# A hybrid attention layer on one core: the seams between the MLP's token blocks, with the last norm's scale, shift and store deferred, a fourth token tile landed early, and the first two weight pieces split apart

## The chip, the cores and the metric

The kernel runs on one core of a Trainium2 chip. The metric is the device time of one execution in microseconds (us), lower is better; where several executions were timed, their median. The engines are named as in the profile: PE is TensorE's matmul (PEld its weight load), DVE is VectorE, ACT is ScalarE, POOL is GpSimd, SP is SyncE, which here only issues DMAs. "ACTq" and "SPq" are DMA issues on the queues of ACT and SP. Each engine works through its own instructions in the order in which they stand.

## The reference

One inference step of one decoder layer in fp32: 2048 prompt tokens and 64 new tokens of 8 running sequences, model width 1024, hidden width 4096. A joint projection feeds softmax attention with forget gates (8 heads of 64; the new tokens read a paged cache of 8192 positions) and an mLSTM (4 heads of 128). Their outputs go through `w_o`, a first layer norm, the MLP and a second one. The part that matters here:

```python
mix = jnp.concatenate([fox_h, mn.astype(x.dtype)], axis=-1) @ w_o
x1 = _layer_norm(DN_ALPHA * x + mix, ln1_g, ln1_b)
hid = jnp.square(jax.nn.relu(x1 @ w1))
return _layer_norm(DN_ALPHA * x1 + hid @ w2, ln2_g, ln2_b)
```

`_layer_norm` subtracts the mean, divides by the root of variance plus epsilon, multiplies by `g` (the scale) and adds `b` (the shift).

## The kernel before, in words

Every large product is done in three passes (`mm3`): both operands are split into a rounded upper half (`split_hi`, an ACT copy, L149) and the rest (`split_lo`, a DVE subtraction, L152), and PE adds upper × upper (L157), upper × lower (L158) and lower × upper (L159). So each weight piece that arrives by DMA (`wr`, 512 KB) costs one ACT operation (`wh`) and one DVE operation (`wl`) before PE can use all of it, and each token tile likewise (`x1h`, `x1l`).

The work comes in phases: the projection, the mLSTM, prompt attention, phase O (`w_o` and the first norm for 16 tiles of 128 prompt tokens; it stores x1 to a scratch tensor, `dx` in the profile and `dx1` in the code) and phase C, the MLP. Phase C takes the tokens in four blocks: tiles 0 to 3, 4 to 7, 8 to 11, and 12 to 15 with the 64 new tokens as a fifth tile, numbered 16. I call the passages between them O→C, 0→1, 1→2 and 2→3. In each block all weights pass once, in 16 slices of 256 hidden columns:

- `hidden(fc)` takes two w1 pieces of 512 rows each (`w1_pieces`), accumulates `ph` in PSUM on PE, and makes relu (ACT, L1392), square (ACT, L1393) and the split of the result (`hh` on ACT, `hl` on DVE). `hq`, the buffer between relu and split, has one copy; `ph` has three, shared with the transposes of token tiles.
- `output(fcs)` takes w2 pieces of 128 rows, accumulates `py` on PE for each tile and half of the columns, and DVE adds it to the tile's output row `y` (L1420 for the first slice, which loads the row from x1 by a DMA on ACT's queue, L1409; L1422 for the others). There are five output rows of 128 x 1024.
- After the last slice `layer_norm` follows tile by tile: statistics on DVE (L165 to L167, L169), a power on POOL (L168), the normalisation on ACT (L170), the scale on DVE (L171), the shift on POOL (L172), and the store to `y_prompt` on SP (L1426).

While the last slice of a block runs, `load(ci + 1)` brings the next block's token tiles: a load on SP into one of two landing buffers (`xr`, L1213), eight transposes on PE (L1225), and the splits into `x1h` and `x1l`, which have one copy each for 576 tokens.

Raw weights have four buffers, which the norms' vectors `g` and `b` also use; `wh` has five and `wl` four.

Beside all this the new tokens' attention over the cache runs in steps (`tick`): indirect DMA gathers issued by POOL (`kT`, `vt`, `xr`), DVE transposes of the keys, short matmuls (`sQ`, `sT`, `sO`) and a custom DVE operation for the scores (L1633).

The code's order isn't the engines' order. A tile scheduler estimates when each instruction can start and orders every engine's queue by that and by priority, with dependences through buffers kept; `tc.issue_after` ties what stands in its scope behind a given instruction.

Of the kernel before, what the change touches and what calls it, by code (L numbers as in the profile page):

```python
# [10 lines left out]
F32 = mybir.dt.float32  # L11
# [3 lines left out]
OP = mybir.AluOpType  # L15
# [37 lines left out]
def body(ctx, tc, I, O, stages):  # L53
# [49 lines left out]
    last = {}  # L103
# [56 lines left out]

    def layer_norm(x, np_, g, b, wk, tg, eng=None):
        w = wk.tile([128, 64], F32, name="ln", bufs=2)
# [7 lines left out]
        A.activation(x, x, AF.Identity, bias=rs[:np_, 2:3], scale=rs[:np_, 1:2])  # L170
        V.tensor_tensor(x, x, g[:np_], op=OP.mult)  # L171
        (eng or G).tensor_tensor(x, x, b[:np_], op=OP.add)  # L172

# [1004 lines left out]
    def landing(n=128):  # L1178

        return pcw.tile([128, 1024], F32, name="xr", bufs=2)[:n]  # L1180
# [9 lines left out]
    C = {}  # L1190
# [13 lines left out]
    def row():  # L1204
        return C["py"].tile([128, D], F32, name="y", bufs=5)

    def w1_pieces(fc):
        return [piece(I["w1"][0][kg * 512:kg * 512 + 512, fc * 256:fc * 256 + 256].rearrange("(k p) c -> p k c", p=128)) for kg in range(2)]
# [21 lines left out]
    def phase_o(halves):  # L1230
# [94 lines left out]
        x1_turn(3, 3, nx[3], px_of)  # L1325
        C["w1"] = w1_pieces(0)
        end(15)
# [4 lines left out]
    def phase_c():  # L1332
# [30 lines left out]

        CB = [[0, 1, 2, 3], [4, 5, 6, 7], [8, 9, 10, 11], [12, 13, 14, 15, 16]]
        def load(ci):
# [4 lines left out]
        vx["more"] = landing  # L1370
        for ci, blk in enumerate(CB):
            W = sum(tok_n(t) for t in blk)
# [25 lines left out]
            def output(fcs):  # L1398
# [4 lines left out]
                for t in blk:  # L1403
# [20 lines left out]
                    if 15 in fcs and t < 16:  # L1424
                        layer_norm(ys[t], n, *gb, pc, "2")
                        SY.dma_start(O["y_prompt"][0, t * 128:(t + 1) * 128], ys[t])  # L1426
# [430 lines left out]
```

## Time and profile before

| | |
|---|---|
| median of 3 executions | 3372.51 us (3365.42 to 3375.61) |
| the profiled execution | 3382.94 us, its span 3381.2 us, mean granted clock 0.988 |
| PE busy | 3266.7 us, 97% of the span |
| DVE busy | 2145.9 us, 63% |
| ACT busy | 1413.8 us, 42% |
| POOL busy | 869.5 us, 26% |
| moved by DMA | 646.25 MB |

Phase C takes the span from about 1617 us to the end. An instruction's row in the profile gives its start, its duration, engine, line, and output and input tiles without their numbers; square brackets hold how long the engine had been idle before it and what released it.

### The profile page before, as it was taken

The page shows a single profiled execution, that of the slowest core. Times are in us where ns is not written, and L with a number is a line of the kernel's source. Part 1 is how long each engine was busy: PE and PEld are TensorE (multiplying, and loading weights), DVE is VectorE, ACT ScalarE, POOL GpSimd, SP SyncE. Part 2 cuts the span into 40 slices and gives each one's busy share as a digit, 9 for nine tenths or more (in the row PEclk, how much of TensorE's full clock was granted, in tenths as well). Part 3 has the DMA queues.
Part 4 walks back from the last instruction along what each step waited for, and adds up shares of the span by engine and source line. Part 5 has one row for each costly group of instructions (what it writes and reads, how often), then busy time and mean ns, then how long its engine had stood idle before and what let it go on. Part 6 is the DMA issues. An engine that isn't in the chain of part 4 may idle for free. (4 is left out here: it accounts for less than half of the span.)

```text
span 3381.2 us, 57759 instructions
## 1 busy us (share of the span) xinstructions
PE 3266.7 (97%) x21564; PEld 2623.4 (78%) x21564; DVE 2145.9 (63%) x5180; ACT 1413.8 (42%) x2989; POOL 869.5 (26%) x928
## 2 busy tenths in 40 slices
PE   9999999999999999999999999999999999999998
PEld 8998897787866667677777776777777777888886
DVE  5857567556478878655666667666676545644545
ACT  4444245334378888422332333232332323433332
POOL 0112122422332222365423324323243110100001
PEclk9999999999999999999999999999999999999999
DMA  5665765866652322587776768767678545532221
GB/s 172 165 189 179 221 206 180 292 212 219 227 166 81 90 76 61 209 283 245 286 249 244 247 226 299 254 234 270 209 258 289 198 164 160 168 103 83 87 76 66
DMA packets 427232, 646.25 MB, mean 191 GB/s; under 512 B 83148, under 2 KB 320016, under 8 KB 426056
## 3 DMA queue, kind: packets, MB, share of 16 engines
q1 hardware_dynamic: 350184, 363.22, 35.3%
q0 software_dynamic: 74304, 270.57, 21.8%
q10 hardware_dynamic: 2464, 8.78, 0.7%
q8 instruction: 170, 2.79, 0.3%
q14 instruction: 110, 0.90, 0.1%
HBM read 589.63 MB, written 52.83 MB: 190 GB/s over the span
## 5 line engine op out<-in xcount | busy, mean ns | idle before, releaser
L1422 DVE TENSOR_TENSOR y<-y,py 128x512 f32<-128x512 f32 (+1 forms) x475 | 320.5, 681 | 310.7 <-PE py L159 287.4
L149 ACT ACTIVATE wh<-wr 128x1024 fp32r<-128x1024 f32 x268 | 278.1, 1056 | 500.8 <-PE py L159 215.3
L159 PE MATMUL ph<-x1h,wl 128*128 128x512 f32 (+1 forms) x1280 | 452.9, 355 | 7.7 <-DVE wl L152 7.1
L157 PE MATMUL ph<-x1h,wh 128*128 128x512 f32 (+1 forms) x1280 | 454.9, 355 | 3.6 <-ACT wh L149 2.9
L1597 POOL DMA_INDIRECT kT<-cache_k,idxK x256 | 272.5, 1064 | 718.2 <-PE sQ L1626 657.7
L158 PE MATMUL ph<-x1l,wh 128*128 128x512 f32 (+1 forms) x1280 | 454.4, 355 | 0.0
L1603 DVE STREAM_TRANSPOSE kT<-kT 128x512 f32<-128x512 f32 x512 | 330.3, 685 | 177.1 <-DMA kT<-cache_k,idxK 170.5
L157 PE MATMUL py<-wh,hh 128*128 128x512 f32 (+1 forms) x1088 | 431.7, 399 | 6.8 <-DVE y L1420 4.0
L158 PE MATMUL py<-wl,hh 128*128 128x512 f32 (+1 forms) x1088 | 426.4, 392 | 0.6 <-issue 0.6
L159 PE MATMUL py<-wh,hl 128*128 128x512 f32 (+1 forms) x1088 | 426.3, 393 | 0.3 <-issue 0.3
L152 DVE TENSOR_TENSOR wl<-wr,wh 128x1024 fp32r<-128x1024 f32 x268 | 335.0, 1256 | 81.5 <-ACT wh L149 28.6
L157 PE MATMUL pm<-whi,xhT 128*128 128x256 f32 (+2 forms) x1088 | 319.0, 293 | 4.6 <-ACT whi L149 1.7
L158 PE MATMUL pm<-wlo,xhT 128*128 128x256 f32 (+2 forms) x1088 | 313.8, 289 | 0.8 <-DVE wlo L152 0.8
L159 PE MATMUL pm<-whi,xlT 128*128 128x256 f32 (+3 forms) x1088 | 313.5, 288 | 0.0
L157 PEld LDWEIGHTS ph<-x1h,wh 128*128 128x128 f32 x1280 | 241.8, 189 | 42.9 <-issue 5.2
L159 PEld LDWEIGHTS ph<-x1h,wl 128*128 128x128 f32 x1280 | 241.8, 189 | 43.0 <-DVE wl L152 9.4
L158 PEld LDWEIGHTS ph<-x1l,wh 128*128 128x128 f32 x1280 | 241.9, 189 | 36.9 <-issue 4.1
L157 PEld LDWEIGHTS py<-wh,hh 128*128 128x128 f32 (+1 forms) x1088 | 201.3, 185 | 64.4 <-issue 11.9
L159 PEld LDWEIGHTS py<-wh,hl 128*128 128x128 f32 (+1 forms) x1088 | 200.9, 185 | 52.7 <-issue 5.3
L158 PEld LDWEIGHTS py<-wl,hh 128*128 128x128 f32 (+1 forms) x1088 | 201.4, 185 | 40.6 <-issue 2.3
L157 PEld LDWEIGHTS pm<-whi,xhT 128*128 128x128 f32 (+1 forms) x1088 | 207.9, 191 | 13.7 <-issue 7.8
L1072 ACT ACTIVATE S<-S,mx 128x512 f32<-128x512 f32 (+2 forms) x320 | 207.8, 652 | 17.7 <-DVE mx L1060 16.6
(394 smaller groups left out, 6534.9 us busy)
## 6 DMA issues: line engine op xcount, KB each, us to landing
wr<-w SPq DMA_DIRECT2D x256, 512.0 KB
wra<-w_in SPq DMA_DIRECT2D x112, 512.0 KB
Rb<-dR SPq DMA_DIRECT2D x128, 128.0 KB
wr<-w_o SPq DMA_DIRECT2D x16, 512.0 KB
xr<-dmix SPq DMA_DIRECT2D x16, 512.0 KB
y<-x_prompt SPq DMA_DIRECT2D x16, 512.0 KB
dx<-y SPq DMA_DIRECT2D x16, 512.0 KB
xr<-dx SPq DMA_DIRECT2D x16, 512.0 KB
```

The costliest lines, as they stand in the source:

```text
L149: last["ACT"] = A.activation(dst, src, AF.Copy, scale=scale)
L152: r = (eng or V).tensor_tensor(dst, src, hi.bitcast(F32), op=OP.subtract)
L157: T.matmul(ps, wh, xh, start=first, stop=False)
L158: T.matmul(ps, wh, xl, start=False, stop=False)
L159: last["PE"] = T.matmul(ps, wl, xh, start=False, stop=stop)
L1072: last["ACT"] = A.activation(sp[:, :w], sp[:, :w], AF.Exp, bias=mx[:, 7:8], accum_out=lp[:, k:k + 1])
L1422: V.tensor_tensor(y, y, ps, op=OP.add)
L1597: G.indirect_dma_start(out=piece(n), out_offset=None, in_=ck, in_offset=IO(ap=idxK[:, b, j // 2, j % 2:j % 2 + 1], axis=0))
L1603: V.transpose(x, x)
```

## The change

Three edits, and a helper for each.

1. `layer_norm` takes a list `later`. If it is given, the scale (DVE) and the shift (POOL) are put there as a function and not run. The MLP's last norm hands it over and puts the store behind them. The next block's first `hidden(0)` runs the list after it has asked for its first two w1 pieces. The last block runs it at once. The operations and bytes are the same.
2. At slice 14 of blocks 0 to 2 the fourth token tile of the next block is loaded into a free output row (`row()`) and not into a landing buffer; `load` takes it from there.
3. In phase O the first two w1 pieces are asked for one by one, and the second one's instructions are tied behind the last `split_lo` of the token tiles.

```diff
-    def layer_norm(x, np_, g, b, wk, tg, eng=None):
+    def layer_norm(x, np_, g, b, wk, tg, later=None):
...
         A.activation(x, x, AF.Identity, bias=rs[:np_, 2:3], scale=rs[:np_, 1:2])
-        V.tensor_tensor(x, x, g[:np_], op=OP.mult)
-        (eng or G).tensor_tensor(x, x, b[:np_], op=OP.add)
+
+        def scale():
+            V.tensor_tensor(x, x, g[:np_], op=OP.mult)
+            G.tensor_tensor(x, x, b[:np_], op=OP.add)
+        scale() if later is None else later.append(scale)
...
+    def w1_piece(fc, kg):
+        return piece(I["w1"][0][kg * 512:kg * 512 + 512, fc * 256:fc * 256 + 256].rearrange("(k p) c -> p k c", p=128))
...
-    def x1_load(t):
-        x = landing()
+    def x1_load(t, x=None):
+        x = landing() if x is None else x
...
         x1_turn(3, 3, nx[3], px_of)
-        C["w1"] = w1_pieces(0)
+        behind = last["DVE"]
+        C["w1"] = [w1_piece(0, 0)]
+        with tc.issue_after(behind.ins):
+
+            C["w1"].append(w1_piece(0, 1))
...
         def load(ci):
             for i, t in enumerate(CB[ci]):
-                x1_turn(t, i, x1_load(t), lambda: ppc.tile([128, 4, 128], F32, name="px2", tag="ph", bufs=3))
+                x1_turn(t, i, ahead.pop(i) if i in ahead else x1_load(t), lambda: ppc.tile([128, 4, 128], F32, name="px2", tag="ph", bufs=3))
...
             def hidden(fc):
                 w1p = C.pop("w1", None) or w1_pieces(fc)
+
+                while later:
+                    later.pop(0)()
...
                     if 15 in fcs and t < 16:
-                        layer_norm(ys[t], n, *gb, pc, "2")
-                        SY.dma_start(O["y_prompt"][0, t * 128:(t + 1) * 128], ys[t])
+                        layer_norm(ys[t], n, *gb, pc, "2", later)
+                        later.append(lambda t=t, y=ys[t]: SY.dma_start(O["y_prompt"][0, t * 128:(t + 1) * 128], y))
+                        while ci == 3 and later:
+                            later.pop(0)()
...
                 if fc == 14:
                     vx["more"] = None
+                    if ci < 3:
+
+                        ahead[3] = x1_load(CB[ci + 1][3], row())
```

The order of the engines' queues is the same up to the end of phase O. From there the scheduler orders all of phase C anew, mostly in small ways. Lines of the changed kernel are a little higher: the scale is L174 there, the first add L1437, the later ones L1439, relu L1409, a `y` load L1426.

**O→C, DVE.** `wl_193xx` are lower halves of the w1 pieces of slice 1, `wl_19282` that of the second piece of slice 0, `wl_195xx` those of w2; `px_19252` to `px_19266` are the last three half tiles of block 0's tokens; `y_19003` is the last row of norm 1. Before:

```order
2888 L1633 ISA S_19227,mxs_18575<-sQ_19210,Rb_19084 128x4x32
2889 L1633 ISA mxs_18575 128x1
2890 L167 TENSOR_SCALAR ln_19285<-ln_19285 128x1
2891 L152 TENSOR_TENSOR wl_19393<-wr_19390,wh_19392 128x1024
2892 L152 TENSOR_TENSOR wl_19399<-wr_19396,wh_19398 128x1024
2893 L152 TENSOR_TENSOR x1l_19100<-px_19252,x1h_19099 128x4x128
2894 L152 TENSOR_TENSOR x1l_19100<-px_19259,x1h_19099 128x4x128
2895 L152 TENSOR_TENSOR x1l_19100<-px_19266,x1h_19099 128x4x128
2896 L169 TENSOR_SCALAR ln_19285<-ln_19285 128x1
2897 L171 TENSOR_TENSOR y_19003<-y_19003,g1_17516 128x1024
```

And now:

```order
2889 L1655 ISA mxs_18575 128x1
2890 L170 TENSOR_SCALAR ln_19285<-ln_19285 128x1
2891 L152 TENSOR_TENSOR x1l_19100<-px_19252,x1h_19099 128x4x128
2892 L152 TENSOR_TENSOR x1l_19100<-px_19259,x1h_19099 128x4x128
2893 L174 TENSOR_TENSOR y_19003<-y_19003,g1_17516 128x1024
2894 L152 TENSOR_TENSOR x1l_19100<-px_19266,x1h_19099 128x4x128
2895 L152 TENSOR_TENSOR wl_19282<-wr_19279,wh_19281 128x1024
2896 L152 TENSOR_TENSOR wl_19393<-wr_19390,wh_19392 128x1024
2897 L152 TENSOR_TENSOR wl_19399<-wr_19396,wh_19398 128x1024
2898 L152 TENSOR_TENSOR wl_19508<-wr_19505,wh_19507 128x1024
2899 L152 TENSOR_TENSOR wl_19514<-wr_19511,wh_19513 128x1024
```

The three `x1l` stood behind two weight pieces and now stand ahead of five; the last scale of norm 1 moved in among them. On SP the load of `wr_19396`, second piece of slice 1, stood straight behind that of `wr_19390`; now it comes after two loads of the sampled rows, since its buffer is the one that norm 1's scale vector leaves.

**0→1, DVE.** `y_19517` to `y_19602` are block 0's four rows; `wl_23145` and `wl_23151` before, `wl_23133` and `wl_23139` now, are the first two w1 pieces of block 1. Before:

```order
3355 L171 TENSOR_TENSOR y_19517<-y_19517,g2_22912 128x1024
3356 L165 BN_STATS ln_23078<-y_19560 128x6 x2
3357 L1697 COPY PTs_22804<-sT_22805 128x4x4x8
3358 L171 TENSOR_TENSOR y_19542<-y_19542,g2_22912 128x1024
3359 L1422 TENSOR_TENSOR y_19602<-y_19602,py_23089 128x512
3360 L152 TENSOR_TENSOR wl_23145<-wr_23142,wh_23144 128x1024
3361 L166 BN_AGGR ln_23078<-ln_23078 128x2
3362 L152 TENSOR_TENSOR wl_23151<-wr_23148,wh_23150 128x1024
```

And now:

```order
3356 L174 TENSOR_TENSOR y_19517<-y_19517,g2_22912 128x1024
3357 L1719 COPY PTs_22806<-sT_22807 128x4x4x8
3358 L170 TENSOR_SCALAR ln_23029<-ln_23029 128x1
3359 L167 BN_AGGR ln_23072<-ln_23072 128x2
3360 L1439 TENSOR_TENSOR y_19602<-y_19602,py_23080 128x512
3361 L152 TENSOR_TENSOR wl_23133<-wr_23130,wh_23132 128x1024
3362 L168 TENSOR_SCALAR ln_23072<-ln_23072 128x1
3363 L152 TENSOR_TENSOR wl_23139<-wr_23136,wh_23138 128x1024
3364 L1439 TENSOR_TENSOR y_19602<-y_19602,py_23094 128x512
3365 L166 BN_STATS ln_23122<-y_19602 128x6
3366 L174 TENSOR_TENSOR y_19542<-y_19542,g2_22912 128x1024
```

Two scales stood ahead of the first two weight pieces; now one does, and the second follows them. The third and fourth come after the next pieces. At 2→3 two scales stand ahead of the first `wl`, before and now.

**2→3, ACT.** `y_30658` to `y_30730` are block 3's five rows, loaded from x1; `y_30730` is the fifth, of the 64 new tokens, and takes the buffer of block 2's last row after its store. Before:

```order
2143 L1409 DMA y_30712<-dx1_72 128x1024
2144 L1392 ACTIVATE hq_30475<-ph_30450 128x288
2145 L149 ACTIVATE wh_30750<-wr_30748 128x1024
2146 L1393 ACTIVATE hq_30475<-hq_30475 128x288
2147 L149 ACTIVATE hh_30448<-hq_30475 128x288
2148 L1392 ACTIVATE hq_30505<-ph_30480 128x288
2149 L1393 ACTIVATE hq_30505<-hq_30505 128x288
2150 L149 ACTIVATE hh_30448<-hq_30505 128x288
2151 L1392 ACTIVATE hq_30549<-ph_30524 128x288
2152 L1393 ACTIVATE hq_30549<-hq_30549 128x288
2153 L149 ACTIVATE hh_30522<-hq_30549 128x288
2154 L1409 DMA y_30730<-dx1_72 64x1024
```

And now:

```order
2146 L1426 DMA y_30712<-dx1_72 128x1024
2147 L149 ACTIVATE hh_30448<-hq_30475 128x288
2148 L149 ACTIVATE wh_30750<-wr_30748 128x1024
2149 L1426 DMA y_30730<-dx1_72 64x1024
2150 L1409 ACTIVATE hq_30505<-ph_30480 128x288
2151 L1410 ACTIVATE hq_30505<-hq_30505 128x288
2152 L149 ACTIVATE hh_30448<-hq_30505 128x288
2153 L1409 ACTIVATE hq_30549<-ph_30524 128x288
```

The load of the fifth row stood behind the relu and split of `hq_30505` and `hq_30549`; now it stands ahead of both.

More of the change, by code (lines that the diff above doesn't have):

```diff
@@ L1205, in row @@
         return C["py"].tile([128, D], F32, name="y", bufs=5)
+    def w1_piece(fc, kg):
+        return piece(I["w1"][0][kg * 512:kg * 512 + 512, fc * 256:fc * 256 + 256].rearrange("(k p) c -> p k c", p=128))
     def w1_pieces(fc):
-        return [piece(I["w1"][0][kg * 512:kg * 512 + 512, fc * 256:fc * 256 + 256].rearrange("(k p) c -> p k c", p=128)) for kg in range(2)]
-    def x1_load(t):
-        x = landing()
+        return [w1_piece(fc, kg) for kg in range(2)]
+    def x1_load(t, x=None):
+        x = landing() if x is None else x
         n = tok_n(t)
```

2 lines of the change are left out of this document (added).

## The prediction

> **What bounds the kernel now.** I read the page first, then the list of waits on TensorE (PE), then the seams of the MLP in windows of 5 us.
>
> ```profile
> span 3381.2 us, 57759 instructions
> ...
> PE 3266.7 (97%) x21564; PEld 2623.4 (78%) x21564; DVE 2145.9 (63%) x5180; ACT 1413.8 (42%) x2989; POOL 869.5 (26%) x928
> ```
>
> Every microsecond that PE isn't busy is a candidate: 3381.2 − 3266.7 = 114.5 us, all phases together. The profiled execution took 3382.94 us, 10.4 us more than the median of 3372.51 us; I work out a difference against it and take that off the median. 0.3% is 10 us, about what a measurement of this kernel can tell from no change: the three runs shown lie from 3365.42 to 3375.61.
>
> Of the waits (columns: total us, times, longest):
>
> ```profile
> PE sO L1738 <- DMA vt<-cache_v,idxV: 21.2, 8, 4.6
> PE ph L159 <- DVE wl L152: 7.1, 5, 3.4
> ...
> PE py L157 <- DVE y L1420: 4.0, 3, 1.7
> PE px L1225 <- DVE x1l L152: 3.7, 1, 3.7
> ```
>
> The second and the fourth row are the seams. The first belongs to the sampled rows' gathers, which this change does not touch except by when they fall; the third row comes soon after seam 0→1. Now PE at the seams, each with what released it; the last row is that later place:
>
> ```profile
> 1616.46 0.66 PE L1225 MATMUL px<-ident,xr 128*128 128x128 f32 x4 [3.72 <-DVE x1l L152]
> ...
> 1622.22 0.40 PE L158 MATMUL ph<-x1l,wh 128*128 128x512 f32 x1
> ...
> 1622.45 0.39 PE L159 MATMUL ph<-x1h,wl 128*128 128x512 f32 x1
> ...
> 2058.17 0.80 PE L159 MATMUL ph<-x1h,wl 128*128 128x512 f32 x1 [3.37 <-DVE wl L152]
> ...
> 2490.99 1.06 PE L1225 MATMUL px<-ident,xr 128*128 128x128 f32 x8 [0.96 <-DMA xr<-dx]
> ...
> 2971.86 0.40 PE L159 MATMUL ph<-x1h,wl 128*128 128x288 f32 x1 [2.05 <-DVE wl L152]
> ...
> 2099.71 0.50 PE L157 MATMUL py<-wh,hh 128*128 128x512 f32 x1 [1.70 <-DVE y L1420]
> ```
>
> Two of the rows only give the pitch of a warm 512-column matmul, 0.23 us. So PE stands 3.72 us where phase O becomes block 0 (O→C), 3.37 us at 0→1, 0.96 us at 1→2, and 2.05 us some 35 us into block 3 (2→3). What follows such a stop is in the windows (busy us by engine, then PEclk, DMA share, GB/s):
>
> ```profile
> 1615.00:1620.00 5.00, 3.54 (x12) 2.88 (x13) 2.70 (x4) 1.12 (x3) 3.78 (x5) 0.74 0.74 232
> 1620.00:1625.00 5.00, 5.00 (x22) 4.08 (x21) 0.21 (x1) 1.19 (x2) 4.50 (x5) 0.92 1.03 419
> ...
> 2055.00:2060.00 5.00, 1.83 (x4) 1.49 (x5) 5.00 (x6) 0.00 (x0) 2.03 (x1) 0.77 0.35 115
> 2060.00:2065.00 5.00, 5.00 (x21) 4.07 (x20) 3.02 (x9) 2.31 (x3) 1.11 (x2) 0.89 0.85 293
> 2095.00:2100.00 5.00, 3.30 (x35) 1.93 (x28) 1.64 (x3) 2.81 (x4) 2.67 (x3) 1.00 1.04 368
> ...
> 2970.00:2975.00 5.00, 3.14 (x15) 3.14 (x16) 4.79 (x7) 3.27 (x6) 0.00 (x0) 0.74 0.34 109
> 2975.00:2980.00 5.00, 5.00 (x23) 4.19 (x23) 1.53 (x4) 0.00 (x0) 0.00 (x0) 0.91 0.33 104
> ```
>
> After three of the four stops the granted clock is below 1.00 for two windows. I count what it lost as 5 us times the shortfall: O→C (0.26 + 0.08) × 5 = 1.7 us, 0→1 (0.23 + 0.11) × 5 = 1.7 us, 2→3 (0.26 + 0.09) × 5 = 1.75 us. The stop of 1.70 us at 2099 has 1.00 in its window. Each seam therefore costs its stop and the clock: 5.4, 5.1, 0.96 and 3.8 us, together 15.3 us, or 0.45%. That is nearly all the change can win.
>
> [...]
>
> **O→C, the split of the first weights.**
>
> ```profile
> 1611.12 1.17 DVE L171 TENSOR_TENSOR y<-y,g 128x1024 f32<-128x1024 f32 x1
> ...
> 1613.11 1.21 DVE L152 TENSOR_TENSOR wl<-wr,wh 128x1024 fp32r<-128x1024 f32 x1
> 1614.58 1.22 DVE L152 TENSOR_TENSOR wl<-wr,wh 128x1024 fp32r<-128x1024 f32 x1 [0.26 <-ACT wh L149]
> 1615.72 1.28 DVE L152 TENSOR_TENSOR x1l<-px,x1h 128x512 fp32r<-128x512 f32 x2
> ...
> 1611.38 1.06 ACT L149 ACTIVATE wh<-wr 128x1024 fp32r<-128x1024 f32 x1 [0.55 <-DMA wr<-w]
> 1613.49 1.06 ACT L149 ACTIVATE wh<-wr 128x1024 fp32r<-128x1024 f32 x1 [1.04 <-DMA wr<-w]
> ...
> 1621.65 1.06 ACT L149 ACTIVATE wh<-wr 128x1024 fp32r<-128x1024 f32 x1 [3.89 <-DMA wr<-w]
> ...
> 1639.99 1.06 ACT L149 ACTIVATE wh<-wr 128x1024 fp32r<-128x1024 f32 x1 [8.04 <-DMA wr<-w]
> ...
> 2047.36 1.24 ACT L170 ACTIVATE y<-y,ln 128x1024 f32<-128x1024 f32 x1
> ...
> 1614.42 1.75 SPq L1196 DMA_DIRECT2D wr<-w  x2
> ...
> 1627.41 0.38 SPq L1196 DMA_DIRECT2D wr<-w  x1
> ```
>
> VectorE (DVE) made two lower halves of weights (1613.11, 1614.58), each behind an upper half that ScalarE (ACT) made late since its load was late, before `x1l` at 1615.72. PE stood for that `x1l`, which frees a PSUM tile. In the new order `x1l` follows the sampled rows' scores directly, at 1613.11, and ACT's `x1h` for it follows the upper half of 1611.38, so it is ready. One `x1l` takes 0.64 us (1.28 for two): PE goes on at about 1613.85 instead of 1616.46. It had stopped at 1616.46 − 3.72 = 1612.74, so 1.1 us is left. Then `x1l` of the last half tile stands behind the norm's scale (L171, 1.17 us) of the last token tile, and the `wl` of the second w1 piece behind that. ACT's normalisation of that tile (1.24 us) comes after its two `x1h`, so it ends near 1614.8, the scale near 1616.0, and 0.64 and 1.21 us more make 1617.9. PE needs it four transposes and 12 matmuls after going on, about 1617.2. Left over 1.1 + 0.7 = 1.8 us, under the 2.05 us that lost clock. Gain 5.4 − 1.8 = 3.6 us.
>
> The price: the second piece of the next w1 slice takes the buffer that norm 1's scale vector held, free only after that last scale. So its load issues at about 1616, and the two w2 loads behind it on the SyncE (SP) queue when those `wl` free their buffers, about 1618 in place of 1614.42, into a DMA that is full (1.03 in 1620–1625). How long a load takes there: issued 1614.42, used 1621.65, 7.2 us; issued 1627.41, used 1639.99, 12.6 us. All five `wl` now stand in one run ahead of the transposes and `hl` on DVE, so a late piece holds those too. Cost 0 to 12.6 − 7.2 = 5.4 us; I take 1.1, near the lower end, since PE has four accumulations of hidden columns to do first. Net −2.5 us.
>
> **0→1, the deferred scale, shift and store.**
>
> ```profile
> 2051.41 3.20 DVE L171 TENSOR_TENSOR y<-y,g 128x1024 f32<-128x1024 f32 x1
> 2054.54 0.67 DVE L1422 TENSOR_TENSOR y<-y,py 128x512 f32<-128x512 f32 x1
> 2055.14 2.98 DVE L152 TENSOR_TENSOR wl<-wr,wh 128x1024 fp32r<-128x1024 f32 x1
> ...
> 2051.11 2.41 POOL L172 TENSOR_TENSOR y<-y,b 128x1024 f32<-128x1024 f32 x1
> 2054.70 2.34 POOL L172 TENSOR_TENSOR y<-y,b 128x1024 f32<-128x1024 f32 x1 [1.17 <-DVE y L171]
> ```
>
> Here DVE was full (5.00 of 5 us in 2055–2060) and two operations took 3.20 and 2.98 us where the same kinds took 1.17 and 1.21 above. Both overlap a shift on GpSimd (POOL, L172): POOL ends at 2053.52 and 2057.04, DVE 1.1 us after each; the add with a PSUM operand at 2054.54 is not stretched though POOL runs. In the new order one scale instead of two stands ahead of the first two `wl`. Its shift can't start before the 2051.11 it had, since the gathers ahead of it on POOL stay; 2.41 us later is 2053.5, I take 2053.8, as the next tile's statistics now stand ahead of the scale. The first `wl` runs beside that shift and ends 1.1 us after it, 2054.9. PE wanted it at 2058.17 − 3.37 = 2054.80. I leave 0.4 us of stop with no clock loss: gain 5.1 − 0.4 = 4.7 us. The deferred operations come later on DVE, where room exists (3.02 of 5 us busy in 2060–2065).
>
> [...]
>
> **1→2, the fourth tile's early load.** The 0.96 us stop waited for a load of an x1 tile into a landing buffer (`xr<-dx`). The fourth tile now sits in the fifth row long before, and landing buffers come free earlier. I take −0.9 us; bounds −0.96 and 0.
>
> **2→3, what doesn't move.**
>
> ```profile
> 2954.13 1.58 SPq L1426 DMA_DIRECT2D y_prompt<-y  x1
> ...
> 2966.25 0.52 ACTq L1409 DMA_DIRECT2D y<-dx  x1
> 2966.87 0.41 ACT L1392 ACTIVATE hq<-ph 128x288 f32<-128x288 f32 x1 [4.97 <-PE py L157]
> ```
>
> Block 3's fifth `y` load stands in ACT's queue and waits until the last deferred row is stored. Before: store issued 2954.13, load released 2966.25, 12.1 us, and ACT's next relu had waited 4.97 us; the late upper halves behind it gave PE's 2.05 us. After, the store is still the last of the four, one weight load earlier on SP, and the `y` load stands two relus earlier on ACT. The wait is not removed; it moves to where PE has fewer finished columns ahead. Queued behind the load are a relu, its square and its split, and the relu frees a PSUM tile that PE wants for its next accumulation. Bounds: 3.8 us gained if the store lands in time; if the 4.97 us of ACT become a stop of PE with its clock, 4.97 + 1.75 = 6.7 us, 2.9 more than before. I take 0, since load and store stay the same and the one moves with the other.
>
> **After the seams.**
>
> ```profile
> 2089.47 1.06 ACT L149 ACTIVATE wh<-wr 128x1024 fp32r<-128x1024 f32 x1 [7.62 <-DMA wr<-w]
> ```
>
> ACT waited 7.62 us for a weight here with the DMA at 1.04, and PE lost 1.70 us, part of 4.0. PE will arrive 4.7 us earlier; loads issue as `wl` frees buffers, about 3.3 us earlier (2058.1 to 2054.9). I count +1.3 us, with 0 and 4.7 as bounds.
>
> **Sum.** −3.6 + 1.1 − 4.7 − 0.9 + 0 + 1.3 = −6.8 us: 3382.94 becomes about 3376, and the median 3372.5 about **3365.5 us**.
>
> **Rivals.**
> *All seams close.* Only the 1.1 us at O→C and 0.4 at 0→1 remain and ACT's stall at 2→3 disappears: 4.3 + 4.7 + 0.96 + 3.8 = 13.8 us, 3358.7 us. For it: every cause is a short queue order, all reordered. Against: 2→3's store is still late.
> *The DMA takes it back.* With shares of 1.03 and 1.04 after both big seams PE would only meet the next load sooner. With the bounds 5.4 and 4.7 in place of 1.1 and 1.3 the sum is −6.8 + 4.3 + 3.4 = +0.9: about 3373 us. Against it: in 1620–1625 PE was 5.00 busy beside that full DMA.
> *Slower: ACT stalls on row stores.* Deferred rows are stored later, and each block's `y` loads on ACT wait for them with relus queued behind. If PE pays 6.7 us at 0→1 and at 1→2, and 2.9 more than before at 2→3, that is 16.3 − 6.8 = +9.5: 3382 us. It decides once a store takes longer than the accumulations that PE can still start, two of 24 matmuls at 0.23 us, about 11 us; the 12.1 us is near that. Against: before 2→3 the last load waits for the third tile's store, not the fourth's.
> *The deferral does little,* since the scheduler still puts the first scale ahead of the weights: the order shows one instead of two at 0→1, and at 2→3 the same two as before. The forecast counts that: 0.4 us are left at 0→1, and 2→3 has no gain at its front. If the first `wl` still came a whole scale late, 3.2 us of the 4.7 would go: about 3369 us, inside the range.
>
> **Chances.** Forecast 0.40, all close 0.27, taken back 0.20, ACT stalls 0.13. Faster by over 0.3% (below 3362.4) needs the second, or the good quarter of the first: 0.36. Slower by over 0.3% (above 3382.6) needs the stall at its full price, or moved gathers that add to the 21.2 us: 0.14. Same 0.50. The range runs from all closed, less a margin of 5 us for the spread of the runs, 3354, to the stall, 3382.
>
> **What would show it.** Right: no stop over 2 us and clock 1.00 at the first two seams; `x1l` ahead of the weight pieces; at 0→1 one stretched operation ahead of PE's need. Wrong: PE waits for ACT `hq` or `hl` near 1635 or 2960, a DMA-bound upper half at 1625–1640 over 12 us, or `vt` waits well over 21 us.

## The result, and the profile after

| | before | after |
|---|---|---|
| median, 22 runs each | 3367.70 us (3359.39 to 3375.61) | 3374.59 us (3362.53 to 3384.85) |
| ratio to before | 1 | 1.0022, 95% interval 1.0013 to 1.0031 |

The change makes the kernel slower by 0.22%, about 7.4 us. The forecast was 7 us faster. The time lies inside the forecast's range; the sign is wrong. The kernel before spreads by 16 us over these runs, and its median lies between 3350.73 and 3367.76 us in the comparisons below, so everything is compared as a ratio to runs on the same chip.

The first two lines of the page after:

```profile
span 3379.1 us, 57751 instructions
...
PE 3267.0 (97%) x21564; PEld 2623.1 (78%) x21564; DVE 2141.5 (63%) x5180; ACT 1416.3 (42%) x2989; POOL 875.1 (26%) x928
```

PE works as long as before (3267.0 us against 3266.7). The profiled execution of before (3382.94 us) lies 15 us above the median of its 22 runs, so the two spans are not compared; the seams are. The waits on PE after the change (total us, times, longest):

```profile
PE sO L1760 <- DMA vt<-cache_v,idxV: 16.4, 6, 4.8
PE py L157 <- DVE y L1437: 8.2, 3, 3.7
PE px L1232 <- DMA xr<-dx: 7.1, 1, 7.1
```

The two rows of before that were the seams, `ph <- DVE wl` (7.1 us) and `px <- DVE x1l` (3.7), are no longer near the top. In their place stand a wait for an add into `y` (8.2; before 4.0 at the same place of the code, L1420) and one single wait of 7.1 us for an x1 tile's load. Here are PE's stops seam by seam: two at O→C with a third 20 us later, two at 0→1, three at 1→2, one at 2→3:

```profile
1602.97 0.66 PE L1232 MATMUL px<-ident,xr 128*128 128x128 f32 x4 [1.23 <-DVE x1l L152]
...
1618.46 0.50 PE L159 MATMUL ph<-x1h,wl 128*128 128x512 f32 x1 [0.76 <-DVE wl L152]
...
1639.23 0.50 PE L157 MATMUL py<-wh,hh 128*128 128x512 f32 x1 [3.75 <-DVE y L1437]
...
2049.01 0.50 PE L159 MATMUL ph<-x1h,wl 128*128 128x512 f32 x1 [0.45 <-DVE ln L168]
...
2082.91 1.93 PE L1648 MATMUL sQ<-kT,qb 128*32 128x256 f32 x32 [1.90 <-issue]
...
2487.84 1.94 PE L1232 MATMUL px<-ident,xr 128*128 128x128 f32 x8 [7.14 <-DMA xr<-dx]
...
2538.81 0.50 PE L157 MATMUL py<-wh,hh 128*128 128x512 f32 x1 [2.57 <-DVE y L1437]
...
2543.76 0.50 PE L157 MATMUL py<-wh,hh 128*128 128x512 f32 x1 [1.93 <-DVE y L1437]
...
2954.14 0.96 PE L157 MATMUL py<-wh,hh 128*128 128x512 f32 x3 [2.06 <-ACT wh L149]
```

And the windows of 5 us behind them (busy us by engine, PEclk, DMA share, GB/s):

```profile
1615.00:1620.00 5.00, 4.24 (x19) 3.15 (x18) 2.10 (x2) 3.13 (x4) 2.31 (x1) 1.00 1.03 420
...
1635.00:1640.00 5.00, 1.25 (x6) 0.66 (x5) 2.64 (x4) 3.67 (x5) 3.81 (x4) 0.97 1.02 392
1640.00:1645.00 5.00, 5.00 (x18) 3.56 (x17) 4.38 (x14) 0.09 (x1) 1.61 (x2) 0.69 1.03 374
...
2045.00:2050.00 5.00, 4.55 (x22) 3.60 (x21) 5.00 (x8) 2.36 (x3) 3.24 (x2) 1.00 0.34 107
...
2480.00:2485.00 5.00, 0.70 (x4) 0.24 (x2) 2.77 (x5) 1.54 (x2) 0.00 (x0) 0.78 1.04 412
2485.00:2490.00 5.00, 2.16 (x10) 2.19 (x11) 5.00 (x11) 0.78 (x2) 0.00 (x0) 0.50 0.21 68
2490.00:2495.00 5.00, 5.00 (x18) 4.07 (x18) 3.96 (x8) 2.09 (x3) 1.51 (x2) 0.70 0.29 105
```

0→1 is closed as forecast: 0.45 us where 3.37 us stood, and full clock. 1→2 has opened: where before PE stopped 0.96 us for a tile's load, it stops 7.14 us, and the clock loses (0.22 + 0.50 + 0.30) × 5 = 5.1 us more (before, the windows from 2480 to 2505 us all have 1.00). That is 11 us worse in one place. SP's queue shows what differs, first before:

```profile
2478.09 0.59 SPq L1196 DMA_DIRECT2D wr<-w  x1
2478.78 0.55 SPq L1213 DMA_DIRECT2D xr<-dx  x1
2479.38 0.50 SPq L1196 DMA_DIRECT2D wr<-w  x1
...
2481.17 2.31 SPq L1213 DMA_DIRECT2D xr<-dx  x1
```

and after:

```profile
2468.67 2.75 SPq L1200 DMA_DIRECT2D wr<-w  x2
2471.53 0.45 SPq L1220 DMA_DIRECT2D xr<-dx  x1
```

Before, the third tile's load went out at 2478.78, between the new block's first two weight loads, and the fourth's at 2481.17; after, the third's goes out behind both weights. It is the third tile that PE waits for, before and after. It was issued at 2471.53 and PE went on at 2487.84, 16.3 us later, with the DMA at 1.03 to 1.04 from 2470 to 2485.

### The profile page after: what moved, and what is told of

Same layout as the page of the kernel before. It is cut to its first block, busy times and chain, and to the rows that moved or that the text cites. A ratio compares the mean times of both kernels' runs of the same rounds, so it can differ in the third digit from the quotient of the medians.

```text
span 3379.1 us, 57751 instructions
## 1 busy us (share of the span) xinstructions
PE 3267.0 (97%) x21564; PEld 2623.1 (78%) x21564; DVE 2141.5 (63%) x5180; ACT 1416.3 (42%) x2989; POOL 875.1 (26%) x928
## 5 line engine op out<-in xcount | busy, mean ns | idle before, releaser
L1439 DVE TENSOR_TENSOR y<-y,py 128x512 f32<-128x512 f32 (+1 forms) x475 | 319.9, 681 | 304.3 <-PE py L159 274.6
L1409 ACT ACTIVATE hq<-ph 128x512 f32<-128x512 f32 (+1 forms) x160 | 82.6, 516 | 335.8 <-PE ph L159 274.8
L1736 POOL DMA_INDIRECT vt<-cache_v,idxV x158 | 163.3, 1033 | 204.9 <-PE sO L1760 142.8
```

What stands on the lines that cost most here:

```text
L1409: A.activation(hq, ps, AF.Relu)
L1439: V.tensor_tensor(y, y, ps, op=OP.add)
L1736: G.indirect_dma_start(out=vt.rearrange("p f c -> p (f c)"), out_offset=None, in_=cv, in_offset=IO(ap=idxV[:, b, (kt % 4) * 4 + kt // 4, f ...
```

## The experiments

The texts on record speak of theories by letters. A lays the loss on the deferral, B on the split, E on the early load; C on nothing but shifted gathers, D on all three edits, whose costs add; F, G and G2 lay it on the scheduler's order at 1→2, H and H2 on the early load itself. They also count ACT's relus (`hq<-ph`) through phase C from 0, 32 to a block in blocks 0 to 2: from relu 16 to 36 lies 0→1, from 48 to 68 or 80 lies 1→2, from 96 to 120 2→3. The stretches are differences of such rows' starts in one profile each; two profiles of the kernel before gave 281.6 and 281.3 us for the first and 443.3 and 443.4 for 48 to 80, but other stretches differ by several us between profiles, so a stretch is a place, and the ratio is the verdict. The piece from relu 80 to 120, with 2→3, took 362 to 368 us in every kernel and decides nothing.

| run | edits (1 deferral, 2 early load, 3 split) | ratio to before, 95% interval | relu 16–36 | relu 48–80 |
|---|---|---|---|---|
| after | 1 2 3 | 1.0022 (1.0013 to 1.0031) | 274.7 | 453.9 |
| e1 | 1 | 1.0002 (0.9990 to 1.0014) | 277.6 | 444.0 |
| e4 | 2 | 1.0022 (1.0012 to 1.0033) | 278.3 | 452.6 |
| e5 | 3 | 0.9995 (0.9981 to 1.0008) | 280.8 | 445.4 |
| e2 | 2 3 | 1.0033 (1.0020 to 1.0047) | 274.2 | 450.6 |
| e6 | 1 3 | 1.0003 (0.9991 to 1.0016) | 281.6 | 447.2 |
| e7 | 1 2 | 1.0017 (1.0004 to 1.0031) | 276.6 | 455.3 |
| e8 | none | 0.9995 (0.9982 to 1.0008) | 281.3 | 443.4 |
| e3 | 1 2 3, SP tied | 1.0023 (1.0011 to 1.0036) | 276.1 | 442.4 |
| e9 | 2, one tie | 1.0017 (1.0007 to 1.0027) | 278.3 | 448.7 |
| e10 | 1 2 3, two ties | 1.0006 (0.9993 to 1.0020) | 275.0 | 447.2 |
| e11 | 1, two ties | 1.0009 (0.9996 to 1.0022) | 281.1 | 450.7 |
| e12 | 2, later | 1.0040 (1.0027 to 1.0054) | 276.3 | 462.6 |
| e13 | 2 at 0→1 only | 1.0003 (0.9988 to 1.0018) | 274.5 | 442.6 |
| e14 | 2 at 0→1 only, one tie | 0.9992 (0.9978 to 1.0006) | 273.5 | 439.4 |
| e15 | 2 at 1→2 only | 1.0038 (1.0025 to 1.0052) | 282.1 | 455.5 |
| e16 | 1, 3, and 2 at 0→1 only, two ties | 1.0010 (0.9998 to 1.0022) | 277.1 | 436.9 |
| e17 | 2, two other ties | 1.0019 (1.0007 to 1.0030) | 276.9 | 450.2 |
| e18 | 2 at 1→2 only, those ties | 1.0028 (1.0012 to 1.0044) | 280.3 | 448.4 |

**Which edit.** Edit 1 undone is the old end of the last norm, edit 2 undone drops the early load, edit 3 undone asks for both w1 pieces at once; against the changed kernel:

```diff
-                        layer_norm(ys[t], n, *gb, pc, "2", later)
-                        later.append(lambda t=t, y=ys[t]: SY.dma_start(O["y_prompt"][0, t * 128:(t + 1) * 128], y))
+                        layer_norm(ys[t], n, *gb, pc, "2")
+                        SY.dma_start(O["y_prompt"][0, t * 128:(t + 1) * 128], ys[t])
...
-                    if ci < 3:
-                        ahead[3] = x1_load(CB[ci + 1][3], row())
...
-        behind = last["DVE"]
-        C["w1"] = [w1_piece(0, 0)]
-        with tc.issue_after(behind.ins):
-            C["w1"].append(w1_piece(0, 1))
+        C["w1"] = w1_pieces(0)
```

e1, the deferral alone:

> Of the three edits only the deferral: scale, shift and store of the last norm run behind the next block's first weight pieces. Theory A (the deferral puts both first w1 pieces of block 2 ahead of the third x1 tile's load on SP, and PE waits for that load): PE stops 6 to 8 us for xr<-dx at 1->2 with the clock low for some 15 us after it, about 11 us; 0->1 gains 5 to 7 us and 2->3 about 3 us; in all +1 to +6 us against before. Theory B (the loss comes from the split of the first weights at O->C, through late loads): no stop over 2 us at 1->2, and -5 to -9 us. Theory C (only sampled gathers have shifted): no pattern, within 3 us of before, stops at sO and sQ.

e2, early load and split without the deferral:

> The early load of the fourth tile and the split of the first weights, without the deferral. Theory A: the 1->2 stop for xr<-dx is 1 us or less again, 0->1 and 2->3 stand as before (3.4 and 2 us), so 0 to +3 us against before, from O->C alone. Theory B: the loss of the whole change is all here, +5 to +9 us, with a stop of 3 to 5 us for y near 25 us after the first relu of block 0. Theory C: anything within 5 us, by where gathers fall.

e4, the early load alone:

> Only the fourth tile's early load into the idle output row. Theory A: 1->2 stop of 0 to 1.5 us, the others as before, -2 to +1 us. Theory B: the same. Theory C: within 4 us. If it is slower by over 4 us, the early loads themselves cost, against all three.

e5, the split alone:

> Only the split of the first two weight pieces. From the end of phase O to the end of the span the runs so far differ by place: with the split, the first four relus after it came 1.7 to 2.6 us later than without. Theory D (each edit only changes in front of what a late first weight stands in an in-order queue, and the edits' costs add): +1 to +4 us against before, with a stop near 4 us for y some 30 us after O->C, and nothing at 1->2. Theory E (the loss is the early load's alone): within 1.5 us of before or faster.

e6, deferral and split without the early load:

> Deferral and split, without the early load of the fourth tile. Theory D: the sum of deferral alone (+0.5) and split alone, +1 to +4 us. Theory E: 0 to +1 us against before; the passage 1->2 takes about 279 us from relu 48 to relu 68 as in before, against 286 to 288 with the early load.

e7, deferral and early load without the split:

> Deferral and early load, without the split. Theory D: the sum of the two alone, +6 to +9 us, less some 2 us than the whole change at O->C. Theory E: +6 to +9 us, 286 us or more from relu 48 to relu 68.

e8, the kernel before once more, as a control:

> The kernel before, unchanged, for a second profile of it on the same chip as its neighbours here: the time within 1.5 us of before (it shows what the comparison can tell). From the end of phase O to the end of the span 1765 to 1775 us; 278 to 280 us from relu 48 to relu 68 if that segment repeats.

The four kernels with the early load took 1.0017 to 1.0033, every interval above 1. The three without it took 0.9995 to 1.0003, as the control did. The loss belongs to edit 2. That is theory E: e5, e6 and e7 came out about as it said. A and B both missed e2, which they had at +9 us at most and which measured about +11, and e4 is slower by over 4 us, which its text had named beforehand as evidence against A, B and C. My first suspicion fell on the deferral, because the 7.14 us stop appears in a weaker form (5.57 and 5.07 us) in both kernels that have the deferral without the early load; but those two kernels are no slower than before. The stop is real and does not decide the total by itself: with edit 2 alone there is no wait for `xr` at 1→2 at all, and the time is the same 1.0022.

**SP's order.** e3 is the whole change with the first two weight loads of blocks 1 to 3 tied behind the last x1 load on SP.

```diff
+        C["ld"] = SY.dma_start(x[:n], dx1[tok_r(t):tok_r(t) + n])
...
+                if w1p is None and fc == 0:
+                    with tc.issue_after(C["ld"].ins):
+                        w1p = w1_pieces(fc)
```

> The whole change, and in hidden(0) of blocks 1 to 3 the first two w1 loads tied behind the last x1 load on SP; nothing else is edited. Theory A: the third x1 tile's load issues some 3 us earlier and without 1 MB ahead of it, the 7.1 us stop at 1->2 falls to 2 us or less without loss of clock, and the time falls by 6 to 11 us against the changed kernel, to 0 to -5 us against before; w1 pieces land later, which may cost up to 3 us of it at a seam. Theory B: no more than 2 us change from the changed kernel, +5 to +9 against before. Theory C: the same as B, or of any sign.

1→2 fell by 11.5 us (453.9 to 442.4), the stop there from 7.14 to 2.21 us, and the ratio stayed at 1.0023. At 0→1 the late weights brought back a stop of 3.92 us for `wl`. The profile's 11.5 us are not found in the time, and I cannot say where all of them went.

**The order on ACT.** With edit 2 alone, the wait at 1→2 is 4.80 us for `py`. There ACT holds the new block's first weight, still waiting for its DMA, ahead of the second tile's `x1h`; before, both `x1h` of that tile stood ahead of it. e9 ties that weight behind the `x1h`.

```diff
+            C["x1h", t] = last["ACT"]
...
+                if w1p is None and fc == 0 and ci == 2:
+                    with tc.issue_after(C["x1h", 9].ins):
+                        w1p = w1_pieces(fc)
```

> Edit 2 alone, with one tie more: in block 2 the first two w1 pieces (their loads, upper and lower halves) are tied behind the second token tile's upper half x1h, so that on ACT the late wh stands behind that x1h again, as in the kernel before. Theory F (the loss at 1->2 is the order: a late weight load's wh stands ahead of x1h on ACT, and y's add stands behind that tile's x1l on DVE): the stop of 4.80 us for py at +215 of the row in edit 2 alone goes, the stretch from relu 48 to relu 68 falls from 288 to about 280 us, and the time to 1.0000 to 1.0010 of the kernel before (edit 2 alone 1.0022). Rival (the loss is what the early load does to the DMA, whatever the order): the stop moves to another weight, the stretch stays at 285 to 289 us, and the ratio at 1.0018 to 1.0030.

The stop for `py` went, as theory F said, but another of 3.33 us for `sQ` stayed 35 us later, and the ratio fell only from 1.0022 to 1.0017, between the two expectations and inside both intervals. e10 puts the tie on SP and on ACT, behind the third tile's load and `x1h` and in block 2 alone, into the whole change; e11 does the same to the deferral alone:

```diff
+        C["ld", t] = SY.dma_start(x[:n], dx1[tok_r(t):tok_r(t) + n])
...
+                if w1p is None and fc == 0 and ci == 2:
+                    with tc.issue_after(C["ld", 10].ins), tc.issue_after(C["x1h", 10].ins):
+                        w1p = w1_pieces(fc)
```

> The whole change, with two ties in block 2 alone: the first two w1 pieces behind the third token tile's load on SP and behind that tile's x1h on ACT. Theory F: the 7.14 us stop for xr at 1->2 and the following 2.57 us stop go, the stretch from relu 48 to relu 68 falls from 286.7 to about 276 to 279 us, the order at 0->1 stays as it was in the change, and the ratio falls from 1.0022 to 0.9990 to 1.0005. Rival (the early load costs through the DMA): at most the 7.14 us stop goes and comes back as a wait for wl in the same stretch; 284 to 288 us, ratio 1.0015 to 1.0025.

> The deferral alone with the same two ties in block 2. Deferral alone had a stop of 5.57 us for xr at 1->2 and 3.4 us of clock behind it, and came out even with the kernel before. Theory F: that stop goes, 5 to 9 us less than the deferral alone, ratio 0.9975 to 0.9988 of the kernel before: faster than both kernels. Rival (the stop is the DMA's, the scheduler gives the time back elsewhere): ratio 0.9995 to 1.0010.

In e10 the 7.14 us stop is 0.49 us:

```profile
2470.36 1.06 PE L1232 MATMUL px<-ident,xr 128*128 128x128 f32 x8 [0.49 <-issue]
```

The ratio is 1.0006 (0.9993 to 1.0020): e10 can't be told from the kernel before. Its interval also overlaps that of the changed kernel (1.0013 to 1.0031), so that most of the loss is gone is what the middle values say and not yet shown; theory F had 0.9990 to 1.0005. In e11 the 5.57 us stop fell to 1.41, but 2.99 us for `hh` and 2.21 for `y` came in its place: 450.7 us against 444.0, and a ratio of 1.0009, so no gain, as the rival there had it.

**When the load goes out.** e12 ties the early load behind the newest weight load, so it leaves late in the block and not at its start (311 and 767 us after phase C's first relu, in place of 16 and 460 in e4).

```diff
+            C["sp"] = SY.dma_start(wr, src)
...
+                        with tc.issue_after(C["sp"].ins):
+                            ahead[3] = x1_load(CB[ci + 1][3], row())
```

> Edit 2 alone, but with the early load of the fourth tile tied behind the weight load asked for last on SP, so that it issues near slice 14 and not at the block's start; the order on ACT at 1->2 is that of edit 2 alone. Theory F (order at the next seam): nothing changes at 1->2, the stretch from relu 48 to relu 68 stays at 285 to 289 us, ratio 1.0015 to 1.0028. Rival (the load at the block's start, into a full DMA, delays weights): the stops near the starts of blocks 1 and 2 shrink and the ratio falls to 1.0000 to 1.0010.

Both expectations were wrong: the ratio is 1.0040, from five runs, with an interval that just overlaps e4's, and 1→2 is 10 us longer. Moving the load away from the busy start of a block thus did not take the loss away; why the later one looks worse I did not find.

**Which seam.** e13 makes the early load for block 1 only (`if ci == 0`), e15 for block 2 only (`if ci == 1`); e14 is e13 with e9's tie; e16 is e10 with `if ci == 0`.

> Edit 2 alone and only at 0->1 (block 1's fourth tile; blocks 2 and 3 load theirs as before). Theory G (a knock-on: the edit at one seam moves the scheduler's order at the next, where ACT gets a late wh ahead of the second tile's x1h; at 1->2 this kernel has that order though nothing is loaded early there): 0->1 gains 3 to 4 us, 1->2 still shows a stop of 4 to 5 us for py behind y's add, the stretch from relu 48 to relu 68 is 286 to 290 us, and the ratio 1.0005 to 1.0025. Rival H (the early load itself costs at 1->2, by its place in the DMA or its buffer): 0->1 gains 3 to 4 us, the stretch stays at 279 to 282 us as before, ratio 0.9980 to 0.9992.

> As the kernel with edit 2 at 0->1 only, and block 2's first two w1 pieces tied behind the second token tile's x1h, which restores the order on ACT there. Theory G: the gain at 0->1 stays, the 4 to 5 us stop at 1->2 goes, the stretch from relu 48 to relu 68 is 279 to 284 us, ratio 0.9980 to 1.0000, the best so far. Rival H: as the kernel without the tie, within 2 us.

> Edit 2 alone and only at 1->2 (block 2's fourth tile). Theories G and H agree on the loss and differ on 0->1 only by what they take away: no gain at 0->1 (stretch from relu 16 to relu 36 280 to 282 us as before), 286 to 290 us from relu 48 to relu 68, nothing at 2->3 (the wait of some 2 us for wh at relu 96 to 104 that all kernels with the edit at 2->3 show is gone, 140 us from relu 96 to 120). G: ratio 1.0015 to 1.0030. H: the same. If the loss were a fixed price of the early load in each block, about a third of 1.0022: 1.0007.

> The whole change with the early load at 0->1 only, and block 2's first two w1 pieces tied behind the third tile's load on SP and its x1h on ACT. Theory G: 0->1 gains 6 us as in the change, 1->2 has no stop over 3 us, 2->3 is as before; from relu 48 to relu 68 275 to 280 us; ratio 0.9980 to 1.0000. Rival (each edit's stop is made up for elsewhere, whatever the order): ratio 1.0003 to 1.0015.

This settles the place between these two seams. The early load at 1→2 alone costs 1.0038; at 0→1 alone 1.0003, and the intervals are apart. In the stretch of 0→1 it even helps (274.5 us against 281.6 and 281.3). At 2→3 alone it was not run. e13 is also a test of the order: nothing is loaded early at 1→2 there, but ACT's order at 1→2 is the new one all the same; presumably the scheduler's clock had moved, which no run shows. The stop for `py` appears in both; first e13, then e15 with its second stop:

```profile
2465.75 0.51 PE L157 MATMUL py<-wh,hh 128*128 128x512 f32 x1 [3.57 <-DVE y L1435]
```

```profile
2477.09 0.79 PE L157 MATMUL py<-wh,hh 128*128 128x512 f32 x1 [5.05 <-DVE y L1435]
...
2514.04 3.33 PE L1642 MATMUL sQ<-kT,qb 128*32 128x256 f32 x32 [4.27 <-issue]
```

So theory G has the first stop right (3.57 us without any early load there) and the loss wrong: e13 is not slower. Rival H missed too, with 0.9980 to 0.9992 for e13. e14 loses the stop and has 0.9992, as G said, but its interval holds e13's 1.0003, so the tie's worth is not shown. e16 has the shortest 1→2 of all (436.9 us) and still 1.0010, where G had 1.0000 at most: its rival, that the time is lost again elsewhere, had 1.0003 to 1.0015.

In the stretch of relu 48 to 80 e15 is 12.1 us longer than before, close to its 0.38%. PE's idle time there is 15.8 us against 7.9 and 6.6 in the two profiles of before, and the clock lost 6.8 us against 1.7 and 3.4, counted as 5 us times the shortfall of each window. So in this profile the loss is PE's stops in that stretch and the clock behind them. Both long stops of e15 have one shape. ACT's and DVE's rows ahead of each:

```profile
2473.58 1.06 ACT L149 ACTIVATE wh<-wr 128x1024 fp32r<-128x1024 f32 x1 [10.74 <-DMA wr<-w]
2474.54 1.06 ACT L149 ACTIVATE x1h<-px 128x512 fp32r<-128x512 f32 x2
...
2475.15 1.29 DVE L152 TENSOR_TENSOR x1l<-px,x1h 128x512 fp32r<-128x512 f32 x2 [6.37 <-ACT x1h L149]
2476.36 1.28 DVE L1435 TENSOR_TENSOR y<-y,py 128x512 f32<-128x512 f32 x2
...
2509.23 1.06 ACT L149 ACTIVATE wh<-wr 128x1024 fp32r<-128x1024 f32 x1 [7.40 <-DMA wr<-w]
...
2510.32 1.22 DVE L152 TENSOR_TENSOR wl<-wr,wh 128x1024 fp32r<-128x1024 f32 x1 [6.19 <-ACT wh L149]
2511.46 2.48 DVE L1619 STREAM_TRANSPOSE kT<-kT 128x512 f32<-128x512 f32 x4
```

A weight's load is late (10.74 us of waiting on ACT), the tile's `x1h` stands behind it, DVE's `x1l` behind that, the add into `y` behind that, and PE waits for the add. The second time a lower half waits, four key transposes stand behind it, and PE's `sQ` wants the transposes; the list calls that wait "issue", and only the neighbouring engine's rows show whose it is.

**Both stops taken away.** e17 (edit 2 at all seams) and e18 (at 1→2 only) add to e9's tie a second one: the weights of block 2's second slice behind the key transposes made last (`KT["turn"]` is the transpose of `k_turn`).

```diff
+                if fc == 1 and ci == 2:
+                    with tc.issue_after(KT["turn"].ins):
+                        w1p = w1_pieces(fc)
```

> Edit 2 at all three seams, with two ties in block 2: its first two w1 pieces behind the second tile's x1h (as once before), and the two w1 pieces of its second slice behind the key transposes made last, so that on DVE four transposes for sQ stand ahead of their two lower halves. Theory G2 (the loss at 1->2 is two stops of one kind: a late weight's upper or lower half with something behind it in ACT's or DVE's order that PE needs sooner): the stop of 3.3 to 4.3 us for sQ at +250 goes too, the stretch from relu 48 to relu 80 falls from 448.7 with the first tie to 441 to 445 us, ratio 0.9995 to 1.0008. Rival H2 (the early load costs at 1->2 in a way that the order of these queues doesn't set): 447 to 454 us, ratio 1.0012 to 1.0025.

> Edit 2 at 1->2 only, with the same two ties. Without them this took 1.0038 [1.0025, 1.0052] of the kernel before, with stops of 5.05 us for py and 4.27 us for sQ. G2: neither stop, 441 to 446 us from relu 48 to relu 80 (455.5 without the ties), ratio 1.0000 to 1.0015, interval apart from 1.0038. H2: 450 us or more, ratio 1.0025 to 1.0040.

The two named stops are gone, and PE now waits as long in the same place for the weights. From e18, ACT, DVE and PE:

```profile
2496.85 1.06 ACT L151 ACTIVATE wh<-wr 128x1024 fp32r<-128x1024 f32 x1 [7.02 <-DMA wr<-w]
...
2507.23 2.31 DVE L154 TENSOR_TENSOR wl<-wr,wh 128x1024 fp32r<-128x1024 f32 x2
...
2508.45 0.80 PE L161 MATMUL ph<-x1h,wl 128*128 128x512 f32 x1 [4.35 <-DVE wl L154]
```

Both weights had their upper halves by 2498, but my tie held the lower ones until 2507.23, behind more transposes than I meant. So these two runs exchange one stop for another: 1.0028 in place of 1.0038 and 1.0019 in place of 1.0022, intervals overlapping. Both ratios lie where H2 had them and above G2's; e18's stretch (448.4 us) lies between the two. Since the tie made a stop of its own, that does not decide between G2 and H2.

**A third wait, on ACT.** One more thing differs at 1→2. Block 2's four `y` loads stand in ACT's queue. Before, they went out together; in e15 the fourth holds ACT until a row of the block before has been stored:

```profile
2524.37 1.92 ACTq L1409 DMA_DIRECT2D y<-dx  x4
```

```profile
2518.75 9.21 ACTq L1422 DMA_DIRECT2D y<-dx  x2
...
2528.07 0.60 ACT L1405 ACTIVATE hq<-ph 128x512 f32<-128x512 f32 x1 [8.59 <-DMA y_prompt<-y]
```

e2, e4, e9 and e12 have the same wait there (8.5 to 9.3 us), and in e17 and e18 the fourth load leaves 13 to 14 us after the third. No kernel without the early load at 1→2 has that wait there, but the changed kernel and e7, which are slower too, don't have it either. PE's stops that follow it in e15 are short (1.14 and 0.86 us), so it is not the larger part. The early tile lies in the fifth output row, and the next block's rows may have to wait for it; no run separates that from the late weights.

**Later scales, later weights.** One row of numbers goes with the early load at 1→2 in most kernels. The norm's vectors `g` and `b` hold two of the four weight buffers until the block's last scale and shift. The last scale of 1→2 and the next weight load on SP, in before and then in e15:

```profile
2518.03 1.22 DVE L171 TENSOR_TENSOR y<-y,g 128x1024 f32<-128x1024 f32 x1
...
2519.27 1.55 SPq L1196 DMA_DIRECT2D wr<-w  x2
```

```profile
2515.95 1.23 DVE L174 TENSOR_TENSOR y<-y,g 128x1024 f32<-128x1024 f32 x1
...
2517.20 0.38 SPq L1200 DMA_DIRECT2D wr<-w  x1
```

In both the load leaves 1.24 or 1.25 us after the scale starts, which is when it ends. Counted from relu 48 (2277.47 and 2259.24) the last scale comes at 240.6 us before and at 256.7 in e15. In e2, e4 and e9 it comes at 252 to 254, in the changed kernel at 249.6, and in e12, the slowest, at 264.4. But it comes at 250.2 in e1, which loses nothing, and at 244 to 246 in e3, e17 and e18, which do lose. That a late scale delays the weight behind it is shown row by row; that late scales are behind the 0.38% is argued only. A kernel with buffers of their own for `g` and `b` would test it and was not run.

No version beats the kernel before beyond the measurement: the best, e14, is at 0.9992 (0.9978 to 1.0006). Set against the changed kernel's 1.0022 it is about 0.3% faster, over two comparisons.

## Why the prediction was wrong, step by step

- **"1→2, the fourth tile's early load": −0.9 us, bounds −0.96 and 0.** This is the step that failed. I priced only a 0.96 us stop, and excluded a loss without a reason. The load that this stop waited for was the third tile's (PE's 17th to 24th transposes of that block), and the edit loads the fourth early, so even the credit was aimed at the wrong tile. Alone and at this seam only, the early load measured a loss of 0.38% or 12.7 us (8.4 to 17.4). In the whole change the seam's front is 11 us worse, but that is not all the early load's: without it e6 still stops 5.07 us there, and the ratio is 1.0003 with that stop and 1.0022 in the whole change. What the rows show in place of the forecast is a changed order: late weights stand ahead of tiles and transposes in the queues of SP, ACT and DVE, and ACT waits for a row store. That this order is the whole price is not shown: two runs made to decide it did not, so the cause behind the loss stays open. I had compared the queues at O→C, 0→1 and 2→3, and never at the seam where I thought little could happen.
- **O→C.** The stops fell to 1.23 + 0.76 = 2.0 us with the clock at 1.00 (1615 to 1620), where 1.8 was forecast: right. The price, taken as 1.1 with 5.4 as its upper end, came out at that end: 3.75 us at 1639.23, and (0.03 + 0.31) × 5 = 1.7 us of clock. The late piece, as foreseen, held what stood behind it on DVE, but that was the add into `y`, not `hl`:

```profile
1636.27 1.06 ACT L149 ACTIVATE wh<-wr 128x1024 fp32r<-128x1024 f32 x1 [6.47 <-DMA wr<-w]
...
1637.36 1.23 DVE L152 TENSOR_TENSOR wl<-wr,wh 128x1024 fp32r<-128x1024 f32 x1 [4.51 <-ACT wh L149]
1638.50 0.68 DVE L1437 SCALAR_TENSOR_TENSOR y<-y,py 128x512 f32<-128x512 f32 x1
```

  So −2.5 was about +2, and the split alone measures 0.9995, no gain.
- **0→1.** Size and end right: 0.45 us left, forecast 0.4, clock 1.00. The credit was half wrong. I had read the order, one scale instead of two ahead of the first two `wl`, as the deferral's doing. In e1 and e6, which defer without the early load, two scales still stand ahead of them, and 1.21 and 1.22 us are left. In e2 and e4, the early load without the deferral, one scale stands ahead and there is no stop for `wl` at all. So the deferral shortens the stop, but the order that I had counted on came with edit 2, and that the size was right is partly luck. And the deferral's gain is not seen in the total: e1 and e6 are at 1.0002 and 1.0003.

```profile
2042.10 0.50 PE L159 MATMUL ph<-x1h,wl 128*128 128x512 f32 x1 [1.22 <-DVE ln L168]
```

- **"After the seams": +1.3.** Some 34 us after the seam PE stops 1.90 us (2082.91), for `sQ`, where before had three stops of 1.38, 1.70 and 0.87 us for `y`: better than forecast.
- **The stretch beside POOL.** The forecast's reading of it at 0→1 held: the first `wl` of block 1 took 2.67 us (from 2046.29) beside a shift that ended at 2047.88, and it ended 1.1 us after that. The `wl` at 2057.44 took 1.21, and the shift beside it 3.37 in place of 2.4. In e6 two `wl` behind deferred scales took 6.74 us together, where one alone takes 1.2, with POOL busy for 4.90 of the 5 us from 2053. The sum has no term for stretches of that kind, and PE had no stop in e6 from 2043 to 2062, so at 0→1 none was needed.

```profile
2052.25 6.74 DVE L152 TENSOR_TENSOR wl<-wr,wh 128x1024 fp32r<-128x1024 f32 x2
```

- **2→3: 0.** One stop of 2.06 us for an upper half, no clock lost, where before had 2.05 us and 1.75 of clock: within its bounds. But the second profile of before (e8) has no stop over 0.8 us there, so the 3.8 us that this seam was priced at are not in every execution.
- **The rivals.** The slower one, ACT stalling on row stores, has the right sign. The changed kernel's ACT shows no wait of over 0.8 us for a row store, so it is not what happened there; but with the early load and without the deferral ACT does wait 8.5 to 9.3 us for a row store at 1→2, with little of it seen on PE. The rival blamed the deferral for it, and the runs show it without. "The DMA takes it back" is nearest at O→C.
- **Clock.** 1→2 lost 5.1 us of clock behind one stop of 7.14 us, over three windows; the 1.7 us that I counted for a stop were seen behind 3.75 us, and nothing behind 2.06.
- **Two slips in the working.** 3372.5 − 6.8 is 3365.7 and not 3365.5, and 0.27 with a quarter of 0.40 makes 0.37 and not 0.36. Nothing hangs on either.

## What to carry to other kernels

Where a scheduler orders in-order queues, a load moved earlier can change the order at later seams too, as it did in e13, and need not be a local saving: compare the queues at each seam, above all at those where you expect little. Check which transfer a stop waited for before you credit an edit with it. Look for a transfer that is still under way with something behind it that the bottleneck needs sooner; a tie that moves one waiter out from behind it may only promote the next. And undo each part alone before reading a story from the largest stop: the longest stop in the profile, 7.14 us, was of a family that two no-slower kernels share.

## What the runs showed of the hardware that I had not expected

Two stops of nearly the same length at the same place of the program, one with and one without a loss of clock. The changed kernel's 2.06 us at 2954.14 has 1.00:

```profile
2950.00:2955.00 5.00, 2.94 (x20) 2.57 (x19) 4.08 (x3) 1.91 (x4) 2.88 (x1) 1.00 0.94 331
2955.00:2960.00 5.00, 5.00 (x39) 4.96 (x38) 2.49 (x4) 4.54 (x9) 0.00 (x0) 1.00 1.07 405
```

and e10's 1.96 us has 0.68:

```profile
2941.57 1.46 PE L157 MATMUL py<-wh,hh 128*128 128x512 f32 x3 [1.96 <-ACT wh L149]
...
2940.00:2945.00 5.00, 3.43 (x13) 3.13 (x14) 3.25 (x4) 4.10 (x7) 0.42 (x1) 0.68 1.03 398
```

So near 2 us, in these profiles, the length of a stop alone does not say whether the clock drops: the first was worth 2.06 us, the second 1.96 + 0.32 × 5 = 3.6. A 512 KB load of a tile took 16.3 us from issue to use (2471.53 to 2487.84), beside seven gathers that POOL issued from 2468.40 to 2477.73 and at a DMA share of 1.03 to 1.04 up to 2485, against the 7.2 and 12.6 us that the forecast had for weights.
